# A two-layer diffusion backbone with an RWKV-7 recurrence: small products reordered over the two halves of the array's rows, and key norms broadcast in one pass

## The chip, the cores and the metric

The kernel runs on one core of a Trainium2 chip. The time is device microseconds from the first to the last instruction of one execution; the median of several runs is compared. One execution was profiled, and every row below is from it.

## The reference

Each of two layers takes a stream of 512 tokens (256 of context, 256 latent) by 1024 channels. Three mixers work on one modulated input: multi-head latent attention, a gated short convolution, and a bidirectional RWKV-7 recurrence with 8 heads of 64 channels. They are projected, gated, summed and projected once more; a SwiGLU feed-forward follows. In the recurrence each head and direction keeps a 64 by 64 state:

```
def step(S, inp):
    r_t, w_t, k_t, v_t, kk_t, a_t = inp
    s_kk = jnp.einsum('bhvk,bhk->bhv', S, kk_t)
    S = S * w_t[:, :, None, :] - s_kk[..., None] * (kk_t * a_t)[:, :, None, :] + v_t[..., None] * k_t[:, :, None, :]
    return S, jnp.einsum('bhvk,bhk->bhv', S, r_t)
```

Here `kk` is the key times `k_k`, divided by its norm over the 64 channels of the head. The decay `w` and the rate `a` come from low-rank products (inner width 64), one pair for each direction:

```
w_log = -jax.nn.softplus(-(w0 + jnp.einsum('btzl,zlc->btzc', jnp.tanh(wd), w_up))) - 0.5
a = jax.nn.sigmoid(a0 + jnp.einsum('btzl,zlc->btzc', ad, a_up))
```

## The kernel before

Channels lie on partitions, tokens along the free axis. Large products take weights as an exact sum of two float32r parts (`wload`, L171: ScalarE rounds, VectorE or GpSimd subtracts), so each is three float32r passes (`mm3`, L198 to L201). A float32 product is two passes on TensorE: it shows as two MATMUL records. A scheduler that models the engines sets the order of instructions on each engine when the program is built; each engine then works through its own list in order and waits on semaphores. Tiles of a pool are handed out in the order of the source: a new tile with a tag waits until the last reader of the old one is done.

The recurrence is worked in chunks of 64 tokens. `rwkv_half` (L897) does 256 tokens (a half) in eight units, one for each head pair `hp` and direction `z`. `stage1` (L930) makes a unit's features. For `z == 0` it broadcasts the key norms over the channels of two heads (L934, `sel` times `rnT`) and loads the low-rank weights, which both directions share; then for each `z` it does the low-rank products over 64 of the array's 128 rows: direction 0 has rows 0 to 63, direction 1 rows 64 to 127 (L955 in layer 0 as float32r triples, L957 in layer 1 as float32). They go to bank `c0` or `c1` in layer 0, and to bank `u` for both directions in layer 1. `stage2` (L981) makes the chunk products: for head `e` of the pair (rows 0 to 63, or 64 to 127) four products in a row, one for each chunk `j`, into one of two banks `G` (L1001 to L1006):

```
for e in range(2):
    ps = pr("G", 2)
    for j in range(4):
        pe.matmul(ps[:, j * 128:j * 128 + ncol], FM[r, j], AR[z][r, e, hp, j, 0:ncol], start=True, stop=True)
```

After the eight units comes the inverse of a triangular matrix: a substitution of 62 VectorE operations (L1040 to L1046), then small TensorE products (L1062, L1074), which take their banks from `y` in layer 1. Then comes the scan over four chunks in both directions (L1106 to L1165): for each chunk and direction `Zs` (L1121, copied at L1124), the correction (L1137, negated at L1138 and L1139), the outputs (L1130, L1144) and the new state (L1158, added at L1159, multiplied at L1163 and L1164). The second half's outputs go to DRAM (`yf`, L1167) and come back for the group norm (`Yf`, L1180, transposed at L1186). The products of the input projection, above all those of the gates (L535), stand between all of this on TensorE; I call them gate products. The attention's operands (`dg` at L642, `cqs` at L637) come after the recurrence.

Of the kernel before, what the change touches and what calls it, by code (L numbers as in the profile page):

```python
# [32 lines left out]
# columns of the packed per-channel vectors  # L33
# [10 lines left out]
# order of the 128-column tiles of w_in: name -> index  # L44
M_CQ, M_CKV, M_KR, M_RW, M_CH, M_CB, M_CC, M_GT = 0, 3, 5, 6, 21, 25, 29, 33
# within the recurrence's tiles
R_WD, R_AD, R_K, R_R, R_V, R_GD = 0, 1, 2, 6, 10, 14
NM_IN = 57
# products begun while the first modulated input is made
# [8 lines left out]
# columns of the output that DVE finishes  # L58
# [16 lines left out]
def body(ctx: ExitStack, tc: tile.TileContext, A: dict, out: bass.AP, dbg=None, upto=None):  # L75
# [12 lines left out]
    def pg():  # L88
        """a bank for a product over weights; a phase may lend banks of its own"""
# [25 lines left out]
    # ---------------------------------------------------------------- constants  # L115
# [4 lines left out]
    sel = ct("sel", [128, 128])  # L120
# [34 lines left out]
    # ---------------------------------------------------------------- DRAM scratch  # L155
# [13 lines left out]
    cnt, share = [0], [3]            # every which piece of weights is split by GpSimd  # L169

    def wload(src, shape, pl=None, tag=None, nb=None, to=None):  # L171
        """one piece of weights into SBUF, split exactly into two float32r parts, 512 columns at a time"""
# [30 lines left out]
    def split(src, hi, lo, scale=None):  # L203
        """hi + lo = src * scale"""
# [8 lines left out]
    # ---------------------------------------------------------------- modulation vectors  # L213
    def mod(ps, l, i, kk, j, pl=None):
        """128 columns of vector i of six (shift, scale, gate of either sub-layer) into the rows of slot j"""
# [7 lines left out]
    def mod_out(ps, n):  # L223
        """rows of partial sums of n slots -> columns [128, slot, stream] without their bias"""
# [9 lines left out]
    def mod_rows(l, i, bank=None):  # L234
        """vector i as rows in DRAM, for the token-major gate"""
# [34 lines left out]
    def to_fm(src, tt, h, xf, dst):  # L270
        """half of the columns, token-major -> modulated, transposed, split"""
# [25 lines left out]
    # ---------------------------------------------------------------- layer norm (token-major) of alpha x + g o  # L297
# [5 lines left out]
    def residual(z, acc, gz, xr, stg):  # L303
        """z = alpha x + g o and its mean, variance and inverse deviation per token"""
# [13 lines left out]
    def post(l, sub, accs, stg, dst, res_in, res_out):  # L318
# [1028 lines left out]
```

## Time and profile before

| | us |
|---|---|
| median of 3 runs | 1935.84 |
| the 3 runs | 1932.49, 1935.84, 1936.29 |
| span of the profiled execution | 1933.0 |
| TensorE busy in it | 1843.0 (95%) |
| VectorE busy | 1189.0 (62%) |
| ScalarE busy | 813.9 (42%) |
| GpSimd busy | 518.9 (27%) |
| mean granted TensorE clock | 0.956 of 2.4 GHz |

The profile gives no other time for the profiled execution than its span, which lies 2.8 us below the median of the runs. A busy TensorE is the time in which some matmul was under way, from its start to its modelled end, so that work that overlaps counts once. In the text "layer 0" ends near 1190 us and layer 1 begins there.

### The profile page before, as it was taken

How to read it: one execution, taken by the hardware profiler on the slowest of the kernel's cores; microseconds unless marked ns; L12 is line 12 of the kernel's file. 1: busy time of each engine (PE TensorE's matmuls, PEld its weight loads, DVE VectorE, ACT ScalarE, POOL GpSimd, SP SyncE). 2: the span in 40 equal slices, each digit the busy share in tenths (PEclk: the TensorE clock that was granted, in tenths of full speed). 3: DMA queues.
4: the chain of work that ended last, by engine and by line, in shares of the span. 5: the costliest groups of instructions: out<-in, count | busy, mean ns of one | idle time of the engine just before them, and what ended most of it. 6: DMA issues, size and time to landing. Idle time of an engine off the chain costs nothing. (4 is left out here: it accounts for less than half of the span.)

```text
span 1933.0 us, 35208 instructions
## 1 busy us (share of the span) xinstructions
PE 1843.0 (95%) x13556; PEld 1507.4 (78%) x13556; DVE 1189.0 (62%) x2202; ACT 813.9 (42%) x1736; POOL 518.9 (27%) x614
## 2 busy tenths in 40 slices
PE   7999999999989999999999998999998999979998
PEld 5877777777767767877888887777787896869996
DVE  4578724974457778633333356598978358875665
ACT  2356333534235443333333223465553355535552
POOL 1467113611124223200000016465522133320001
PEclk9998999899989999999999998987899999989999
DMA  8443444244485427433334324453356474566563
GB/s 329 133 142 112 148 130 134 88 137 129 148 284 196 126 62 243 153 131 131 99 98 142 120 87 156 128 145 118 100 180 192 159 257 138 155 232 228 184 231 118
DMA packets 150728, 300.72 MB, mean 156 GB/s; under 512 B 30433, under 2 KB 85793, under 8 KB 150561
## 3 DMA queue, kind: packets, MB, share of 16 engines
q1 hardware_dynamic: 147584, 289.88, 45.9%
q10 hardware_dynamic: 2976, 8.59, 1.3%
q8 instruction: 107, 1.75, 0.4%
q14 instruction: 61, 0.49, 0.1%
HBM read 261.69 MB, written 36.73 MB: 154 GB/s over the span
## 5 line engine op out<-in xcount | busy, mean ns | idle before, releaser
L188 ACT CAST hi<-raw 128x512 fp32r<-128x512 f32 x548 | 331.4, 617 | 553.5 <-PE pg L200 138.7
L189 DVE TENSOR_TENSOR lo<-raw,hi 128x512 fp32r<-128x512 f32 x454 | 331.8, 737 | 371.4 <-ACT hi L188 353.0
L199 PE MATMUL pg<-xh,hi 128*128 128x512 f32 (+1 forms) x912 | 341.3, 376 | 3.5 <-ACT pp L429 2.5
L200 PE MATMUL pg<-xl,hi 128*128 128x512 f32 (+1 forms) x912 | 335.4, 368 | 0.5 <-DVE xl L207 0.5
L201 PE MATMUL pg<-xh,lo 128*128 128x512 f32 (+1 forms) x912 | 334.3, 367 | 0.0
L201 PE MATMUL p_f<-x2h,lo 128*128 128x256 f32 (+1 forms) x688 | 231.9, 337 | 2.2 <-DVE lo L189 2.2
L199 PE MATMUL p_f<-x2h,hi 128*128 128x256 f32 (+1 forms) x688 | 232.7, 338 | 1.0 <-ACT hi L188 1.0
L200 PE MATMUL p_f<-x2l,hi 128*128 128x256 f32 (+1 forms) x688 | 231.6, 337 | 0.6 <-DVE x2l L207 0.6
L189 POOL TENSOR_TENSOR lo<-raw,hi 128x512 fp32r<-128x512 f32 x94 | 126.2, 1343 | 379.5 <-ACT hi L188 345.2
L199 PEld LDWEIGHTS pg<-xh,hi 128*128 128x128 f32 x912 | 183.8, 202 | 35.5 <-issue 6.3
L200 PEld LDWEIGHTS pg<-xl,hi 128*128 128x128 f32 x912 | 184.1, 202 | 26.3 <-issue 3.2
L201 PEld LDWEIGHTS pg<-xh,lo 128*128 128x128 f32 x912 | 183.8, 202 | 23.6 <-issue 1.1
L295 POOL TENSOR_TENSOR rs<-rs,mhalf 128x1 f32<-128x1 f32 x12 | 9.1, 760 | 580.0 <-DVE rs L314 580.0
L199 PEld LDWEIGHTS p_f<-x2h,hi 128*128 128x128 f32 x688 | 131.5, 191 | 16.0 <-ACT hi L188 2.9
L201 PEld LDWEIGHTS p_f<-x2h,lo 128*128 128x128 f32 x688 | 131.4, 191 | 15.8 <-DVE lo L189 2.5
L200 PEld LDWEIGHTS p_f<-x2l,hi 128*128 128x128 f32 x688 | 131.5, 191 | 13.8 <-DVE x2l L207 0.9
L1006 PE MATMUL p_G<-AR,FM 64*128 64x128 f32 x384 | 54.1, 298 | 7.5 <-POOL lo L189 2.4
L613 POOL TENSOR_TENSOR acc<-acc,gts 128x512 f32<-128x512 f32 (+1 forms) x32 | 38.9, 1224 | 82.7 <-DVE gts L611 71.2
L1006 PEld LDWEIGHTS p_G<-AR,FM 64*128 64x128 f32 x384 | 46.8, 200 | 17.9 <-issue 7.6
L990 POOL TENSOR_TENSOR FM<-ta,di 64x256 f32<-64x256 f32 x64 | 53.9, 842 | 23.7 <-PE p_G L1018 15.7
L220 PE MATMUL pg<-raw,cs 128*32 128x128 f32 x1024 | 56.0, 308 | 2.8 <-DMA raw<-in_modw_dram 1.5
L283 ACT ACTIVATE xf<-p_f,modB,modA 128x128 f32<-128x128 f32 x40 | 17.4, 457 | 85.8 <-PE p_f L276 61.2
(391 smaller groups left out, 3678.5 us busy)
## 6 DMA issues: line engine op xcount, KB each, us to landing
raw<-in_win_dram SPq DMA_DIRECT2D x114, 512.0 KB, 4.4
raw<-in_modw_dram SPq DMA_DIRECT2D x96, 512.0 KB, 4.1
raw<-in_w_dram SPq DMA_DIRECT2D x88, 512.0 KB, 3.6
raw<-in_ffn_w_dram SPq DMA_DIRECT2D x44, 512.0 KB, 4.2
raw<-in_wo_dram SPq DMA_DIRECT2D x24, 512.0 KB, 3.5
raw<-in_w_out_dram SPq DMA_DIRECT2D x16, 512.0 KB, 3.6
feat<-nb SPq DMA_DIRECT2D x25, 256.0 KB, 2.6
gate<-gt SPq DMA_DIRECT2D x24, 256.0 KB, 2.8
```

Of the source, the lines that this page charges most:

```text
L188: act.copy(out=hi, in_=r)
L189: e.tensor_tensor(out=lo, in0=r, in1=hi.bitcast(F32), op=ALU.subtract)
L199: pe.matmul(ps, wh, xh, start=first, stop=False, skip_group_check=True)
L200: pe.matmul(ps, wh, xl, start=False, stop=False, skip_group_check=True)
L201: pe.matmul(ps, wl, xh, start=False, stop=last, skip_group_check=True)
L220: pe.matmul(ps[32 * (k % 4):32 * (k % 4) + 32, 0:128], cs[:, o:o + 32], raw[:, k], start=(j == 0 and k < 4), stop=(k >= 4), skip_group_che ...
L283: act.activation(out=xf[:, kk], in_=pt[:, k * 128:(k + 1) * 128], func=ACTF.Identity, scale=modA[:, kk, z:z + 1], bias=modB[:, kk, z:z + 1])
L295: pool.tensor_tensor(out=out_, in0=in_, in1=e, op=ALU.pow)
L613: pool.tensor_tensor(out=a, in0=a, in1=g, op=ALU.add)
L990: pool.tensor_tensor(out=FM[r, :, k0:k0 + 64], in0=rc(ta[r]), in1=rc(Pi[r]), op=ALU.mult)
L1006: pe.matmul(ps[:, j * 128:j * 128 + ncol], FM[r, j], AR[z][r, e, hp, j, 0:ncol], start=True, stop=True)
```

## The change

The chunk products of a unit take both `G` banks at once and alternate between the two heads, that is between the two halves of the array's rows, the upper rows first; `queue_after` adds a dependence without a semaphore, which holds this order in TensorE's list. The low-rank products of both directions are written where `z == 0` is, alternating too, but without such a dependence; they take two banks, `c0` and `c1` in layer 0, and `u` and `y` in layer 1. The key norms are stored as a rounded part and a remainder in four rows, so that one float32r pass over `sel` with four rows adds them. For this `norms` gains a ScalarE copy and two GpSimd operations on 128 x 8 elements for each head pair, and `sel` is loaded through a float32 tile and rounded once.

```
+    def queue_after(later, earlier):
+        tc.add_manual_dep(later.ins, earlier.ins.name,
+                          mybir.DependencyInfo(mybir.DependencyClass.NoSync, mybir.DependencyReason.DATA),
+                          reason="order of issue")
...
-        pow_mhalf(st["rn"][:, :, hp, 0:2], r, 8)
+        pow_mhalf(r, r, 8)
+        h = st["rnh"][:, :, hp]
+        act.copy(out=h, in_=r)
+        pool.tensor_copy(out=st["rn"][:, :, hp, 0:2], in_=h.bitcast(F32))
+        pool.tensor_tensor(out=st["rn"][:, :, hp, 2:4], in0=r, in1=h.bitcast(F32), op=ALU.subtract)
...
-                pe.matmul(pb[:, 0:HT], sel[32 * hp:32 * hp + 2], rnT[32 * hp:32 * hp + 2, h0:h0 + HT], start=True, stop=True)
+                pe.matmul(pb[:, 0:HT], sel[32 * hp:32 * hp + 4], rnT[32 * hp:32 * hp + 4, h0:h0 + HT], start=True, stop=True)
...
+                pus = [pr("u"), pr("y")] if last else [pr("c0"), pr("c1")]
+                zs = (slice(0, 64), slice(64, 128))
+                for i in range(2):
+                    c = slice(i * HT, (i + 1) * HT)
+                    if U3[l]:
+                        for n, (a, b) in enumerate(((0, 0), (0, 1), (1, 0))):
+                            for q, pu in zip(zs, pus):
+                                pe.matmul(pu[:, c], up[q, a, i], wa[q, i, b], start=(n == 0), stop=(n == 2),
+                                          skip_group_check=True)
+                    else:
+                        for q, pu in zip(zs, pus):
+                            pe.matmul(pu[:, c], up[q, i], wa[i][q], start=True, stop=True)
...
-            zz = slice(64 * z, 64 * z + 64)
-            pu = pr("u" if last else f"c{z}")
-            for i in range(2):
-                o = pu[:, i * HT:(i + 1) * HT]
-                if U3[l]:
-                    mm3(o, up[zz, 0, i], up[zz, 1, i], wa[zz, i, 0], wa[zz, i, 1], True, True)
-                else:
-                    pe.matmul(o, up[zz, i], wa[i][zz], start=True, stop=True)
+            pu = pus[z]
...
+            pgs = [pr("G", 2) for e in range(2)]
+            before = None
+            for j in range(4):
+                for e in (1, 0):
+                    r = slice(64 * e, 64 * e + 64)
+                    i = pe.matmul(pgs[e][:, j * 128:j * 128 + ncol], FM[r, j], AR[z][r, e, hp, j, 0:ncol], start=True,
+                                  stop=True)
+                    if before is not None:
+                        queue_after(i, before)
+                    before = i
```

TensorE, layer 0, the chunk products of the third unit of the first half (`p_G`), before:

```order
L201 MATMUL pg_3868<-xh_243,lo_3861 128x512
L199 MATMUL pg_3868<-xh_243,hi_3860 128x512
L1006 MATMUL p_G_1498<-AR0_1287,FM_1487 128x128 x4
L1006 MATMUL p_G_1507<-AR0_1287,FM_1487 128x128 x4
L1018 MATMUL p_y_1516<-ident_69,FM_1487 128x128 x4
L199 MATMUL p_c1_1594<-wa_1278,uhl_1531 128x256
```

The same unit in the changed kernel, with the low-rank products of direction 1 (`p_c1`) ahead of it:

```order
L206 MATMUL pg_3883<-xl_244,hi_3879 128x512
L966 MATMUL p_c1_1550<-wa_1293,uhl_1546 128x256 x5
L1023 MATMUL p_G_1514<-AR0_1302,FM_1502 128x128
L966 MATMUL p_c1_1550<-wa_1293,uhl_1546 128x256
L1042 MATMUL p_y_1610<-ident_69,FM_1581 128x128
L1023 MATMUL p_G_1513<-AR0_1302,FM_1502 128x128
L1023 MATMUL p_G_1514<-AR0_1302,FM_1502 128x128
L1023 MATMUL p_G_1513<-AR0_1302,FM_1502 128x128
L1023 MATMUL p_G_1514<-AR0_1302,FM_1502 128x128
L1023 MATMUL p_G_1513<-AR0_1302,FM_1502 128x128
L1023 MATMUL p_G_1514<-AR0_1302,FM_1502 128x128
L1023 MATMUL p_G_1513<-AR0_1302,FM_1502 128x128
```

The two banks alternate, but the first product stands alone: a product of another tile shape (L1042, 128 rows) comes before the other seven. The low-rank products of direction 1 stand together, five and one. In all, the chunk products were 42 stretches of 8 passes and 11 of 16; now they are 27 of 2, 26 of 14, 5 of 16, one of 8 and one of 6. Stretches of products over 64 rows, low-rank ones included, were 75 and are 85.

TensorE, layer 1, where the low-rank products of direction 1 for the second half's first head pair stand, before (bank `u`, right behind a chunk product of the first half):

```order
L199 MATMUL pg_14114<-xh_10673,hi_14110 128x256
L1006 MATMUL p_G_12030<-AR0a_11627,FM_12021 128x64 x4
L1121 MATMUL p_c1_12392<-SV1_12338,AR1a_11628 64x64
L957 MATMUL p_u_12912<-twd_12870,lw_12888 128x256
L957 MATMUL p_u_12912<-ad_12872,lw_12888 128x256
```

The same products in the changed kernel (bank `y`, L970), among the scan of the first half (L1161, L1182, L1145):

```order
L1161 MATMUL p_c1_12431<-Zs_12429,LBa_11657 64x64 x5
L1182 MATMUL p_c0_12400<-SV0_12361,tml0_12364 64x64 x8
L1161 MATMUL p_c1_12431<-Zs_12429,LBa_11657 64x64 x2
L970 MATMUL p_y_12920<-twd_12898,lw_12916 128x256
L970 MATMUL p_y_12920<-ad_12900,lw_12916 128x256
L206 MATMUL pg_14912<-xl_10689,hi_14908 128x256
```

They moved behind the first half's inverse, which holds bank `y` before them; seven of the second half's eight units follow there, where before all eight stood ahead of that inverse.

TensorE, layer 1, the end of the second half's scan, before (outputs L1144, then gate products from `xh` and `xl`):

```order
L201 MATMUL pg_15530<-xh_10673,lo_15527 128x256
L1144 MATMUL p_y_14030<-LB_12876,SV1_13923 64x64 x7
L199 MATMUL pg_15530<-xh_10673,hi_15526 128x256
L200 MATMUL pg_15530<-xl_10674,hi_15526 128x256
L201 MATMUL pg_15530<-xh_10673,lo_15527 128x256
```

The same place in the changed kernel (outputs L1168, `dg` of the attention L648, keys from `ch`, then the transposes of `Yf` at L1210):

```order
L1154 MATMUL p_y_14058<-AR1_12903,SV1_13951 64x64 x8
L1168 MATMUL p_y_14058<-LB_12904,SV1_13951 64x64 x8
L648 MATMUL p_G_15953<-dg_15969,ones_70 128x128
L205 MATMUL pg_16000<-hi_15992,ch_15972 128x512
L206 MATMUL pg_16000<-lo_15993,ch_15972 128x512
L205 MATMUL pg_16008<-hi_15992,ch_15972 128x512
L206 MATMUL pg_16008<-lo_15993,ch_15972 128x512
L1210 MATMUL p_y_16258<-ident_69,Yf_16256 128x128 x4
```

The gate products are gone from here: before, 153 of them stood between the last output and the transposes of `Yf`, now none does, and none stands in the scan ahead of it either. They moved to earlier places in layer 1, 293 of them in one stretch ahead of the second half's inverse.

## Rows read from the trace of the kernel before

**Rows 1.** The page: busy time of the engines, and TensorE by slices of 48 us.
```profile
PE 1843.0 (95%) x13556; PEld 1507.4 (78%) x13556; DVE 1189.0 (62%) x2202; ACT 813.9 (42%) x1736; POOL 518.9 (27%) x614
...
PE   7999999999989999999999998999998999979998
```

**Rows 2.** Busy time by stretch of layer 1: PE, PEld, DVE, ACT, POOL, granted clock.
```profile
1300.00:1350.00 50.00, 43.75 (x228) 36.28 (x228) 42.25 (x76) 29.67 (x82) 28.57 (x44) 0.77 0.40 124
1350.00:1400.00 50.00, 46.40 (x268) 37.53 (x267) 47.69 (x94) 24.58 (x58) 24.70 (x35) 0.85 0.31 93
1400.00:1450.00 50.00, 48.01 (x682) 43.90 (x682) 37.12 (x76) 25.86 (x51) 13.23 (x17) 0.93 0.57 178
1450.00:1500.00 50.00, 44.49 (x730) 39.77 (x729) 39.35 (x82) 20.75 (x42) 14.12 (x18) 0.97 0.60 188
1500.00:1560.00 60.00, 60.00 (x910) 50.24 (x909) 22.31 (x48) 20.28 (x47) 11.72 (x12) 1.00 0.47 153
```

**Rows 3.** Timeline of TensorE (start, us, form): both heads' chunk products adjacent.
```profile
130.38 1.71 PE L1006 MATMUL p_G<-AR,FM 64*128 64x128 f32 x16
132.01 0.66 PE L1018 MATMUL p_y<-ident,FM 128*128 128x128 f32 x4
```

**Rows 4.** Timeline of TensorE: one head's chunk products alone.
```profile
159.75 1.16 PE L1006 MATMUL p_G<-AR,FM 64*128 64x128 f32 x8
160.84 0.65 PE L1018 MATMUL p_y<-ident,FM 128*128 128x128 f32 x4
```

**Rows 5.** Timeline of TensorE: two passes over 64 rows between others.
```profile
148.05 0.38 PE L199 MATMUL p_c<-wa,uhl 64*128 64x256 f32 x1
148.27 0.28 PE L200 MATMUL p_c<-wa,uhl 64*128 64x256 f32 x1
148.48 0.50 PE L200 MATMUL pg<-xl,hi 128*128 128x512 f32 x1
```

**Rows 6.** Timeline of TensorE: the two passes of a norm broadcast.
```profile
324.04 0.69 PE L934 MATMUL p_c<-rnT,sel 2*128 2x256 f32 x2
324.66 0.50 PE L200 MATMUL pg<-xl,hi 128*128 128x512 f32 x1
```

**Rows 7.** Timeline of TensorE: sixteen-pass groups of the scan, and gate products.
```profile
303.67 0.69 PE L1158 MATMUL p_c<-SV,TM 128*64 128x64 f32 x16
304.29 0.68 PE L1137 MATMUL p_c<-Zs,LB 64*64 64x64 f32 x16
...
1507.43 0.28 PE L199 MATMUL pg<-xh,hi 128*128 128x256 f32 x1
1507.55 0.28 PE L200 MATMUL pg<-xl,hi 128*128 128x256 f32 x1
```

**Rows 8.** Groups by line and shape: VectorE and ScalarE in the scan (busy, mean ns).
```profile
L1124 ACT COPY Zs<-p_c 128x256 f32<-128x256 f32 x32 | 11.9, 372 | 21.6 <-PE p_c L1121 21.3
L1139 DVE TENSOR_SCALAR SV<-p_c 64x256 f32<-64x256 f32 x32 | 13.7, 428 | 27.4 <-ACT SV L1138 26.8
L1159 DVE TENSOR_TENSOR S<-p_c,S 128x256 f32<-128x256 f32 x28 | 11.9, 424 | 29.3 <-PE p_c L1158 28.9 <-PE p_c L1121 0.2
```

**Rows 9.** Timeline of TensorE: last outputs of the scan, and transposes of `Yf`.
```profile
1558.56 0.68 PE L1144 MATMUL p_y<-LB,SV 64*64 64x64 f32 x14
...
1578.47 0.60 PE L642 MATMUL p_G<-dg,ones 128*128 128x128 f32 x4
1578.91 0.38 PE L1186 MATMUL p_y<-ident,Yf 128*128 128x128 f32 x2
```

**Rows 10.** DMA issues: size each, median us from issue to landing.
```profile
yf<-sq SPq DMA_DIRECT2D x3, 512.0 KB, 5.6
Yf<-yf SPq DMA_DIRECT2D x3, 512.0 KB, 7.6
```

**Rows 11.** Busy time in layer 0's second substitution (columns of rows 2).
```profile
399.00:438.80 39.80, 39.05 (x343) 30.28 (x343) 33.68 (x76) 10.12 (x21) 3.91 (x4) 1.00 0.50 159
```

**Rows 12.** Groups by line and shape: a small GpSimd operation.
```profile
L967 POOL COPY fd<-tw 128x4 f32<-128x4 f32 x32 | 11.1, 347 | 5.2 <-ACT tw L966 4.9
```

More of the change, by code (lines that the diff above doesn't have):

```diff
@@ L119, in body @@
     mask = ct("mask", [128, 320])
-    sel = ct("sel", [128, 128])
+    sel = ct("sel", [128, 128], F32R)
     sv = ct("sv", [128, NL, NV])
@@ L879, in norms @@
             st["rn8"] = rt("rn8", [128, 4, 4, 2])
+            st["rnh"] = rt("rnh", [128, 4, 4, 2], F32R)
             pool.memset(st["rn"], 0.0)
@@ L892, in norms_t @@
             pe.transpose(prt[:, t * 128:(t + 1) * 128], rn[:, t].rearrange("p h e -> p (h e)"), ident)
-        rnT = rt("rnT", [128, T])
+        rnT = rt("rnT", [128, T], F32R)
         dve.tensor_copy(out=rnT, in_=prt)
@@ L946, in stage1 @@
                     up = uhl
-                kks[hp] = (kf, kk, fload(R_R + hp, "rr", 2) if read else None, up)
-            kf, kk, rr, up = kks[hp]
-            rv = (lambda a: a) if z == 0 else (lambda a: a[:, ::-1])
-            zz = slice(64 * z, 64 * z + 64)
-            pu = pr("u" if last else f"c{z}")
-            for i in range(2):
-                o = pu[:, i * HT:(i + 1) * HT]
-                if U3[l]:
-                    mm3(o, up[zz, 0, i], up[zz, 1, i], wa[zz, i, 0], wa[zz, i, 1], True, True)
-                else:
-                    pe.matmul(o, up[zz, i], wa[i][zz], start=True, stop=True)
+                pus = [pr("u"), pr("y")] if last else [pr("c0"), pr("c1")]
[10 more added lines that the diff above has]
+                            pe.matmul(pu[:, c], up[q, i], wa[i][q], start=True, stop=True)
+                kks[hp] = (kf, kk, fload(R_R + hp, "rr", 2) if read else None, pus)
+            kf, kk, rr, pus = kks[hp]
+            rv = (lambda a: a) if z == 0 else (lambda a: a[:, ::-1])
+            pu = pus[z]
             tw = rt("tw", [128, HT], bufs=2)
@@ L1003, in stage2 @@
                 o = slice(64 - 64 * e, 128 - 64 * e)
-                ps = pr("G", 2)
-                for j in range(4):
-                    pe.matmul(ps[:, j * 128:j * 128 + ncol], FM[r, j], AR[z][r, e, hp, j, 0:ncol], start=True, stop=True)
-                p4 = ps.rearrange("p (j t) -> p j t", t=128)
+                p4 = pgs[e].rearrange("p (j t) -> p j t", t=128)
                 act.copy(out=LB[64 * e:64 * e + 32, z, hp, :, 0:64], in_=p4[64 * e:64 * e + 32, :, 0:64])
@@ L1262, in start @@
                     sp.dma_start(out=mask, in_=A["mask"])
-                    sp.dma_start(out=sel, in_=A["sel"])
+                    selw = ip.tile([128, 128], F32, tag="selw", name="selw", bufs=1)
+                    sp.dma_start(out=selw, in_=A["sel"])
+                    act.copy(out=sel, in_=selw)
                 for m in range(len(ws)):
@@ L1318, in pack @@
     sel = np.zeros((4, 32, 128), np.float32)
-    sel[:, 0, :64] = 1.0
-    sel[:, 1, 64:] = 1.0
+    sel[:, 0:4:2, :64] = 1.0
+    sel[:, 1:4:2, 64:] = 1.0
     A["sel"] = sel.reshape(128, 128)
```

## The prediction

> **What bounds the kernel now.** I read the page first. TensorE is busy for 1843.0 of 1933.0 us, and the slices show no stretch where it rests for long [rows 1]. So the time is TensorE's own work and 90 us of idling; a saving in TensorE's passes is a saving in time, unless the new order of work opens a wait. Then the timeline of TensorE, for the price of each kind of small product, and last the busy time by stretch of layer 1, because the order changes most there. Between 1300 and 1500 us TensorE idles for 6.25 + 3.60 + 1.99 + 5.51 = 17.35 us, and its granted clock is between 0.77 and 0.97 of full speed; behind it, at 1500 to 1560, it doesn't idle at all and has full clock [rows 2]. The reader is to see there that layer 1 has one stretch with too little TensorE work and one, the scan and the hand-over, that gate products fill. Prices below are from one start to the next, since durations overlap.
>
> **Chunk products.** Sixteen passes, both heads adjacent, took 132.01 - 130.38 = 1.63 us [rows 3], and eight passes of one head 160.84 - 159.75 = 1.09 us [rows 4]. Two passes over 64 rows took 0.43 us [rows 5]. From 2 to 8 passes that is 0.66 us for 6, 0.11 us a pass, with 0.21 us for entering and leaving the 64-row shape. In single file sixteen would be 0.21 + 16 x 0.11 = 1.97 us; they took 0.34 us less, which is three passes of one half beside three of the other where the heads meet. So the halves do run beside each other, and alternation would make this hold for the whole stretch: fourteen passes are seven on each half, 0.21 + 7 x 0.11 = 0.98 us, and sixteen 1.09 us. I take 1.09 us for both, since the half that starts first can't be used up evenly. Before: 42 x 1.09 + 11 x 1.63 = 63.7 us. After, by the counts of the order: 27 x 0.43 + 26 x 1.09 + 5 x 1.09 + 1.09 + 0.87 = 47.4 us (8 passes at their single-file price, 6 likewise). The term is **-16.3 us**. At worst alternation gains no more overlap than the meeting heads have, fourteen passes at 0.21 + 14 x 0.11 - 0.34 = 1.41 us and sixteen at 1.63: 58.4 us and a gain of 5.3. The lone first product of 27 units costs 27 x 0.21 = 5.7 us of the gain; it is in the sum.
>
> Of the Trainium skill, "TensorEngine Tiling (Array Packing)", section "Key Properties", says that different tiles load weights and multiply in parallel, but also that a change of the tiling mode drains TensorE. The trace agrees with the first by the 1.63 us above, and its 0.21 us at the ends of a stretch fits the second. By the drain alone, with the passes in single file, this change would lose: the order has 85 such stretches where there were 75, and the chunk products would take 27 x 0.43 + 26 x 1.75 + 5 x 1.97 + 1.96 = 68.9 us, 5.2 more than now; that is the far end of rival D.
>
> **Norm broadcasts.** Sixteen of them, of two passes each, become one pass. A pair took 324.66 - 324.04 = 0.62 us [rows 6]; half of it is 0.31 us, 16 x 0.31 = **-5.0 us**. If only the pass and none of the entering went, it would be 16 x 0.12 = 1.9, taking 0.12 us as the price of a 256-column pass [rows 7]. The ScalarE copy and two GpSimd operations for each head pair and layer cost TensorE nothing where gate products are at hand: a GpSimd copy of four columns took 0.35 us [rows 12], and the three are a chain of some 1.1 to 1.5 us, once for each layer ahead of `norms_t`. Without cover that would be 3 us in all. The rounding of `sel` is one copy under the first products.
>
> **Low-rank products.** The order realises almost no alternation (six of `c0`, then six of `c1`; in layer 1 a pair of each). I take **-2 us** for fewer broken stretches. The bounds are 0, and full alternation: in layer 0 four head pairs in two halves, six passes of 0.12 us each hidden [rows 7], 8 x 0.72 = 5.8 us; in layer 1 eight times four float32 passes of 256 columns, at twice the 0.11 us of 128 columns [rows 4], 7.0 us; together 12.8. The shown order speaks for the low end.
>
> The three make **-23.3 us**.
>
> **What layer 1 gives back.** There bank `y` is held by the first half's inverse, so seven of the second half's units come behind it, and with them the second scan and the hand-over come later than all gate products.
>
> *The naked scan.* A step's chain is 0.68 + 0.37 + 0.68 + 0.43 + 0.69 + 3 x 0.42 = 4.1 us: two correction products [rows 7], the copy, the negation, the state product, and one addition and two multiplications, all at the addition's price [rows 8]. With hand-overs I estimate 4.4 us. TensorE's work for both directions of a step is ten groups of 0.62 us [rows 7], 6.2 us, so the directions can cover each other, and three inner steps lose little; the first step and the last have no partner. I take **+5 us**, bounds 3 (one chain less what the other direction covers) and 10 (over two chains bare).
>
> *The hand-over.* Before, the last outputs started at 1558.56 us and the transposes of `Yf` at 1578.91 [rows 9], with 153 gate products of 0.12 us, 18.4 us, between. After, the `yf` store (5.6 us) and the `Yf` load (7.6 us) [rows 10] stand bare: 13.2 us, and a little for the copy ahead. TensorE has `dg` and four key products for it, some 2.4 us by pass prices. **+11 us**; 7 if the keys' weights give it more, 13 if these wait too. What is late next is the group norm, and the scores behind it on TensorE.
>
> *The second substitution.* In layer 0 one took 39.8 us with VectorE at 33.68 [rows 11]. In layer 1 after, 293 gate products of 0.12 us, 35.2 us, stand ahead of the inverse, and some products of the late units: **+2 us**, 0 to 6.
>
> *The clock.* At 1300 to 1350 the idling of 6.25 us goes with a granted clock of 0.77, that is with stretches at 1.2 instead of 2.4 GHz [rows 2]. After a bare wait of 11 us small work follows. **+3 us**; none at the least, and 13 if it is as in that window (there 11.5 of 50 us lost).
>
> *The credit.* The gate products that no longer stand in scan and hand-over stand earlier, where TensorE idled for 17.35 us and ran below full clock [rows 2]. Work moved into a wait costs nothing: of these 17.35 us I credit **-13 us**, not all, since VectorE is nearly the limit in a part of it (47.69 of 50 us at 1350). Bounds 0, and 29 with half of the 24 us that the lower clock took there, 50 x (0.23 + 0.15 + 0.07 + 0.03).
>
> Layer 1 thus gives back 5 + 11 + 2 + 3 - 13 = 8 us, and the sum is -15.3 us: 1917.7 us against the profiled 1933.0. That execution lies 2.8 us under the median of the runs, so I forecast 1920.5, **1920 us**.
>
> **The rivals.** A change within 0.2% (3.9 us) is about what a measurement of this kernel can tell from none.
>
> *A, the forecast*, 0.50: alternation as priced, layer 1 gives back 8 us, more or less 11: 1909 to 1931.
>
> *B, nothing is given back*, 0.22. The gate products that move into the idle stretch, and the better clock there, pay for scan and hand-over whole: 1935.8 - 23.3 = 1912. With the credit at 29 it is 8 us less, 1904, and about 1898 with more of the low-rank products alternating. For it speak the 17.35 us of idling and the 24 us of lost clock [rows 2]; against it 13.2 us of transfers that nothing shortens [rows 10]. I put it at 1905.
>
> *C, slower*, 0.14: from the second scan to the transposes of `Yf` the work is one dependent chain, bare and at 1.2 GHz, and what moved ahead of it buys little, because VectorE and not TensorE's list sets the pace at 1300 to 1500. At their bounds the chain's terms are 10 + 13 + 13, with 2 for the substitution 38 us, and the time 1935.8 - 23.3 + 38 = 1950. It decides from where give-back less credit passes 23.3 + 3.9 = 27 us, that is with a credit below 11. VectorE's 47.69 of 50 us at 1350 speaks for it, its 37.12 at 1400 against [rows 2].
>
> *D, it doesn't do what it says*, 0.14: alternating passes overlap no more than adjacent heads did. 5.3 for the chunk products, 5.0 and 2 for the others, 8 given back: 1935.8 - 12.3 + 8 = 1931.5, and 1933.5 without the low-rank part. In single file it would be 1942. Against it stands the overlap where the heads meet [rows 3].
>
> The range of 1900 to 1938 leaves out C and the lower end of B, some 2 in 10. Faster by over 0.2% holds A but for 0.02, B, and half of D: 0.77; within 0.2% 0.10; slower 0.13.
>
> **What the profile after would show.** Stretches of chunk products of 14 passes at about 1.0 to 1.1 us from start to start (D: 1.4), the broadcast line with 16 instead of 32 passes, TensorE's busy time some 20 us lower. In layer 1: fewer idle us and a higher clock where the first half's substitution is, then a second scan without gate products, TensorE idle for some 11 us ahead of the `Yf` transposes, released by the load of `Yf`, and a granted clock below 1 behind it. The forecast fails if a stretch of 14 takes 1.4 us or more, or if the stretch at 1300 to 1500 idles as long as before although it has more gate products.

## The result, and the profile after

The changed kernel took 1955.97 us (median of 4 runs, 1952.28 to 1957.24) beside 1936.07 us for the kernel before (4 runs): a ratio of 1.0096, with a 95% interval of 1.0068 to 1.0124. It is slower, by some 20 us, where 1920 us and a gain were forecast; 1955.97 us lies outside the range too. Of the rivals C, the slower one at 1950 us, came nearest.

The page after: busy time of the engines, and TensorE by slices of 49 us, beside [rows 1].

```profile
PE 1816.6 (93%) x13540; PEld 1483.6 (76%) x13540; DVE 1200.9 (61%) x2202; ACT 812.5 (42%) x1745; POOL 526.3 (27%) x630
...
PE   7998999999979999999999999899898788979998
```

TensorE is busy for 26.4 us less than before, somewhat more than the 23.3 us that the sum took off. But the span is 1954.1 us, so it idles for 137.5 us where it idled for 90.0. The work went, and more waiting came. The timeline of TensorE shows that the prices were right: sixteen passes of chunk products alternating (1.10 us from start to start, 1.63 before), fourteen (1.09 us), and a norm broadcast (0.31 us).

```profile
122.76 0.38 PE L945 MATMUL p_c<-rnT,sel 4*128 4x256 f32 x1
123.07 0.50 PE L205 MATMUL pg<-xh,hi 128*128 128x512 f32 x1
...
129.85 1.16 PE L1023 MATMUL p_G<-AR,FM 64*128 64x128 f32 x16
130.95 0.66 PE L1042 MATMUL p_y<-ident,FM 128*128 128x128 f32 x4
...
156.45 1.16 PE L1023 MATMUL p_G<-AR,FM 64*128 64x128 f32 x14
157.54 0.55 PE L1042 MATMUL p_y<-ident,FM 128*128 128x128 f32 x3
```

So the two halves do run beside each other. Of the Trainium skill, "TensorEngine Tiling (Array Packing)", section "Key Properties", has both the parallel tiles and the drain; the 1.10 us agree with the first, and the second did not take the gain away: a stretch of fourteen is at 1.09 us, not at the 1.75 us of rival D's far end. In all, the 512 passes took 67.5 us before and 49.8 us after, from start to next start and without idle time, so 17.7 us less where 16.3 were forecast.

Busy time by stretch of layer 1 after (columns as in [rows 2]):

```profile
1300.00:1350.00 50.00, 46.51 (x321) 39.51 (x319) 33.69 (x68) 26.16 (x67) 19.06 (x25) 0.91 0.45 148
1350.00:1400.00 50.00, 44.46 (x615) 41.73 (x616) 36.47 (x70) 23.30 (x44) 11.55 (x12) 0.93 0.55 185
1400.00:1450.00 50.00, 43.87 (x447) 36.44 (x448) 45.77 (x76) 24.88 (x65) 29.25 (x46) 0.80 0.42 125
1450.00:1500.00 50.00, 45.24 (x496) 38.09 (x492) 32.01 (x54) 23.80 (x60) 22.99 (x33) 0.97 0.57 179
1500.00:1560.00 60.00, 47.09 (x574) 44.95 (x573) 45.80 (x89) 26.46 (x51) 14.48 (x11) 0.87 0.59 183
```

Between 1300 and 1500 us TensorE idles for 19.92 us (17.35 before), although it has more gate products there (586 passes, before 513), and for 12.91 us in the 60 us behind, where it had not idled. The first of these is one of the two signs by which the prediction itself said that it would fail.

Where the time went is seen by a few starts on TensorE. First the kernel before: the last product of layer 0, the first of layer 1's second inverse, the last gate product; the last outputs of the scan and the transposes of `Yf` are in [rows 9].

```profile
1162.61 0.39 PE L201 MATMUL p_f<-late,hh 128*128 128x512 f32 x1
...
1487.36 0.82 PE L1062 MATMUL p_y<-sq,LB 32*32 32x32 f32 x40
...
1588.71 0.28 PE L201 MATMUL pg<-xh,lo 128*128 128x256 f32 x1
```

The same in the changed kernel, with the last outputs and the transposes:

```profile
1155.44 0.39 PE L207 MATMUL p_f<-late,hh 128*128 128x512 f32 x1
...
1540.71 0.28 PE L207 MATMUL pg<-xh,lo 128*128 128x256 f32 x1
...
1546.68 1.92 PE L1086 MATMUL p_y<-sq,LB 32*32 32x32 f32 x64 [5.70 <-DVE sq L1072]
...
1587.83 1.14 PE L1168 MATMUL p_y<-LB,SV 64*64 64x64 f32 x16 [0.46 <-ACT SV L1162]
...
1599.47 1.05 PE L1210 MATMUL p_y<-ident,Yf 128*128 128x128 f32 x4
```

Layer 0 ends 7.2 us earlier. From there the second inverse begins after 391.2 us, in the kernel before after 324.8: 66.5 us later. From the inverse to the last outputs it takes 41.2 us, before 71.2, because no gate product stands between; from those to the transposes 11.6 us, before 20.4. So the bare scan and the bare hand-over, which I had priced as losses, are 39 us shorter than the covered ones, and the loss was made ahead of them, where I had put a credit. At the transposes layer 1 is 27.7 us behind, and at the end 28.3: 28.3 - 7.2 = 21.1 us of span.

The order on bank `y` shows the place: the last low-rank product of direction 1 for the first half, then the first half's inverse, and behind it the second half's.

```profile
1278.89 0.38 PE L970 MATMUL p_y<-twd,lw 64*128 64x256 f32 x1
1379.03 1.20 PE L1086 MATMUL p_y<-sq,LBa 32*32 32x32 f32 x64 [0.61 <-DVE sq L1072]
...
1395.62 1.20 PE L1098 MATMUL p_y<-LBa,sq 32*32 32x32 f32 x64
1402.32 0.70 PE L970 MATMUL p_y<-twd,lw 64*128 64x256 f32 x2
```

For 123 us no low-rank product of direction 1 is issued. That is what the order showed before; what it costs is read from VectorE. First the kernel before, while the first half's substitution runs; then the changed kernel, the same substitution, and the stretch from the first half's inverse to the second half's substitution (columns as in [rows 2]; VectorE is the third).

```profile
1331.60:1409.30 77.70, 68.58 (x413) 56.07 (x412) 73.51 (x149) 38.82 (x96) 36.80 (x52) 0.87 0.39 118
```

```profile
1332.80:1376.80 44.00, 36.47 (x328) 33.22 (x327) 35.98 (x84) 15.21 (x33) 9.58 (x9) 0.92 0.58 195
1402.30:1502.60 100.30, 89.40 (x924) 75.14 (x921) 79.60 (x131) 50.16 (x128) 52.24 (x78) 0.88 0.50 156
```

Before, the second half's units were made while the substitution ran: beside its own 62 operations, other operations of VectorE, 55.0 us in all, lie in its 77.7 us, and VectorE is nearly full. After, 13.7 us of others lie in its 44.0 us, and the work of seven units follows behind the inverse, in a stretch that is not full (79.60 of 100.30 us). The second substitution starts 347.2 us after layer 0's last product, before 270.8.

### The profile page after: what moved, and what is told of

It is laid out like the page before. It is cut to its first block, busy times and chain, and to the rows that moved or that the text cites. A ratio compares the mean times of both kernels' runs of the same rounds, so it can differ in the third digit from the quotient of the medians.

```text
span 1954.1 us, 35135 instructions
## 1 busy us (share of the span) xinstructions
PE 1816.6 (93%) x13540; PEld 1483.6 (76%) x13540; DVE 1200.9 (61%) x2202; ACT 812.5 (42%) x1745; POOL 526.3 (27%) x630
## 3 DMA queue, kind: packets, MB, share of 16 engines
q8 instruction: 107, 1.75, 0.4%
## 5 line engine op out<-in xcount | busy, mean ns | idle before, releaser
L195 DVE TENSOR_TENSOR lo<-raw,hi 128x512 fp32r<-128x512 f32 x454 | 339.4, 753 | 354.2 <-ACT hi L194 348.6
L205 PE MATMUL pg<-xh,hi 128*128 128x512 f32 (+1 forms) x912 | 335.0, 369 | 14.2 <-DVE modT L258 5.5
L206 PE MATMUL pg<-xl,hi 128*128 128x512 f32 (+1 forms) x912 | 329.9, 362 | 1.2 <-DVE xl L213 1.2
L206 PEld LDWEIGHTS p_f<-x2l,hi 128*128 128x128 f32 x688 | 132.1, 192 | 13.7 <-DVE x2l L213 1.0
L1007 POOL TENSOR_TENSOR FM<-ta,di 64x256 f32<-64x256 f32 x64 | 55.2, 862 | 24.8 <-PE p_G L1042 17.6
L1004 DVE SCALAR_TENSOR_TENSOR FM<-bp,di 64x256 f32<-64x256 f32 x64 | 47.3, 740 | 12.5 <-PE p_G L1042 8.9
L289 ACT ACTIVATE xf<-p_f,modB,modA 128x128 f32<-128x128 f32 x40 | 17.6, 457 | 85.1 <-PE p_f L282 65.8
L1070 DVE TENSOR_TENSOR sq<-sq,iv 128x31 f32<-128x31 f32 (+15 forms) x124 | 50.5, 407 | 3.1
```

What stands on the lines that cost most here:

```text
L195: e.tensor_tensor(out=lo, in0=r, in1=hi.bitcast(F32), op=ALU.subtract)
L205: pe.matmul(ps, wh, xh, start=first, stop=False, skip_group_check=True)
L206: pe.matmul(ps, wh, xl, start=False, stop=False, skip_group_check=True)
L289: act.activation(out=xf[:, kk], in_=pt[:, k * 128:(k + 1) * 128], func=ACTF.Identity, scale=modA[:, kk, z:z + 1], bias=modB[:, kk, z:z + 1])
L1004: dve.scalar_tensor_tensor(out=FM[r, :, b0:b0 + 64], in0=v4(bp[r]), scalar=0.5, in1=v4(Pi[r]), op0=ALU.mult, op1=ALU.mult)
L1007: pool.tensor_tensor(out=FM[r, :, k0:k0 + 64], in0=rc(ta[r]), in1=rc(Pi[r]), op=ALU.mult)
```

## The experiments

Theories, numbered as the expectations use them: (1) bank `y`, taken by direction 1 in layer 1, holds the second half's units back. (2) A unit that claims both `G` banks at once is slower. (3) The norms' longer chain delays the units. (4, 5) VectorE, or the recurrence's chain through it, sets the pace, so passes saved there are worth little. (6) The dependence that pins the alternation makes the first head wait for the second. (7) The wrong head comes first. (8) Layer 1 has a second limit right behind TensorE's work: the recurrence's end and a fixed tail.

Ratios are to the kernel before, run on the same chip in turn. All times in the table but the ratios are of the profiled execution: the start of layer 0's last product, the span from there on ("layer 1"), the starts of layer 1's second inverse (its first TensorE product) and of the last group of scan outputs, and the span from these to the end ("tail").

| kernel | ratio (95%) | span | layer 0 | layer 1 | inverse | outputs | tail |
|---|---|---|---|---|---|---|---|
| before | 1 | 1933.0 | 1162.6 | 770.4 | 1487.4 | 1558.6 | 374.4 |
| changed | 1.0096 (1.0068 to 1.0124) | 1954.1 | 1155.4 | 798.7 | 1546.7 | 1587.8 | 366.3 |
| e1_chunks | 1.0007 (0.9985 to 1.0028) | 1940.7 | 1164.1 | 776.6 | 1500.1 | 1575.0 | 365.7 |
| e2_norms | 0.9980 (0.9958 to 1.0002) | 1937.3 | 1163.4 | 773.9 | 1486.6 | 1561.6 | 375.7 |
| e3_lowrank | 1.0080 (1.0050 to 1.0110) | 1969.3 | 1163.1 | 806.2 | 1526.2 | 1599.5 | 369.8 |
| e4_u_in_layer1 | 0.9994 (0.9972 to 1.0015) | 1936.8 | 1160.7 | 776.1 | 1487.6 | 1562.2 | 374.6 |
| e5_both_banks | 1.0042 (1.0020 to 1.0064) | 1934.8 | 1162.7 | 772.1 | 1481.7 | 1559.1 | 375.7 |
| e6_t_in_u | 1.0089 (1.0054 to 1.0125) | 1949.5 | 1155.7 | 793.8 | 1498.8 | 1575.4 | 374.2 |
| e7_before_t_in_u | 1.0075 (1.0048 to 1.0101) | 1946.6 | 1160.5 | 786.1 | 1494.7 | 1570.0 | 376.6 |
| c1_chunks_norms_u | 1.0101 (1.0070 to 1.0132) | 1956.8 | 1168.4 | 788.4 | 1504.4 | 1581.3 | 375.5 |
| e8_g3_layer0 | 1.0067 (1.0040 to 1.0095) | 1944.5 | 1167.4 | 777.1 | 1501.9 | 1576.7 | 367.8 |
| e12_twice | 1.0306 (1.0269 to 1.0342) | 1996.4 | 1171.4 | 825.0 | 1507.2 | 1579.5 | 416.9 |
| e13_norms_share2 | 0.9958 (0.9936 to 0.9980) | 1928.9 | 1154.5 | 774.4 | 1475.2 | 1552.5 | 376.4 |
| e14_noqueue | 0.9935 (0.9913 to 0.9958) | 1923.5 | 1151.5 | 772.0 | 1475.1 | 1546.3 | 377.2 |
| f1_after_noqueue | 1.0053 (1.0028 to 1.0078) | 1952.1 | 1165.2 | 786.9 | 1532.5 | 1588.0 | 364.1 |
| f2_noqueue_u | 1.0009 (0.9987 to 1.0031) | 1938.0 | 1163.8 | 774.2 | 1482.2 | 1560.1 | 377.9 |
| e10_order01 | 1.0082 (1.0053 to 1.0110) | 1949.8 | 1171.4 | 778.4 | 1507.0 | 1581.5 | 368.2 |
| f3_best | 1.0035 (1.0013 to 1.0058) | 1955.5 | 1170.1 | 785.4 | 1503.4 | 1581.0 | 374.5 |
| e17_gates_two | 1.0001 (0.9981 to 1.0020) | 1932.3 | 1158.3 | 774.0 | 1488.6 | 1564.7 | 367.6 |
| f6_noqueue_share | 0.9997 (0.9980 to 1.0014) | 1936.7 | 1147.7 | 789.0 | 1469.8 | 1550.5 | 386.2 |

A profiled execution can lie 10 to 15 us from its kernel's median (e5_both_banks took 1936.6 us in it, with a median of 1947.1; e3_lowrank 1971.1, with a median of 1956.0), so the ratio gives the verdict and the columns only the place.

### The parts one by one

e1_chunks: the kernel before with the diff's part in `stage2`.

> Only the chunk products alternate; low-rank products and norm broadcasts as before. Theory 1 (the bank y, which low-rank direction 1 takes in layer 1, makes the second half's units wait for the first half's inverse): the saving of 16 us shows nearly whole, 12 to 18 us faster than before, about 1920; the two halves' inverses in layer 1 stay some 70 us apart. Theory 2 (a unit takes both G banks at once, so units follow one another more slowly): 0 to 15 us slower than before, with idle TensorE ahead of chunk products and transposes in layer 1.

e2_norms: the diff's parts in `norms`, `norms_t`, `sel`, and the broadcast of four rows.

> Only the norm broadcast in one pass. Theories 1 and 2 alike: 2 to 5 us faster than before, about 1931 to 1934. Theory 3 (the longer chain of ScalarE and GpSimd ahead of the transposed norms delays all units): 3 to 10 us slower than before.

e3_lowrank: the low-rank products of the diff.

> Only the low-rank products, both directions written together, with bank y for direction 1 in layer 1. Theory 1: all of the loss is here: 30 to 45 us slower than before, 1965 to 1980, with the second scan and the hand-over bare of gate products. Theory 2: within 5 us of before.

e4_u_in_layer1: the whole diff, but

```diff
-                pus = [pr("u"), pr("y")] if last else [pr("c0"), pr("c1")]
+                pus = None
+                if not last:
+                    pus = [pr("u"), pr("y")] if last else [pr("c0"), pr("c1")]
...
-            pu = pus[z]
+            pu = pus[z] if pus else pr("u" if last else f"c{z}")
```

> The whole change, but in layer 1 the low-rank products stand as before (bank u for each direction in its turn). Theory 1: the loss goes and the savings stay: 20 to 28 us faster than before, about 1910 to 1916. Theory 2: about as the changed kernel, 1950 to 1956.

Theory 1 holds for the loss: with the low-rank products alone, `y` among them, the second inverse is at 1526.2 us (e3) and the time 0.80% longer; with everything but `y` the whole 0.96% is gone. The expected 30 us and more of e3 was too much, and the savings of 20 us and more did not show in e4: TensorE is busy for 1817.5 us there, 25.5 less than before, and the time is the same. Theory 3 falls. But neither theory has e1: alternation alone takes 23.1 us off TensorE's busy time (1819.9 us) and gives nothing. Its two inverses in layer 1 stay 71 us apart, as theory 1 has it, but both come 13 us later. One unit of it, in the timeline of TensorE:

```profile
1373.37 0.48 PE L1011 MATMUL p_G<-AR,FM 64*128 64x128 f32 x2
...
1375.17 1.16 PE L1011 MATMUL p_G<-AR,FM 64*128 64x128 f32 x14
...
1382.71 1.09 PE L1030 MATMUL p_G<-ident,FM 128*128 128x128 f32 x4 [3.38 <-DVE AR L1026]
```

The first head's first product stands alone, fourteen passes follow when the other head is ready, and the transposes, which need a `G` bank, wait until VectorE has emptied one: 9.3 us after the unit's first product.

### Why the chunk products give nothing

e5_both_banks keeps the claim and a pinned order, but not the alternation:

```diff
-            for j in range(4):
-                for e in (1, 0):
+            for e in (1, 0):
+                for j in range(4):
```

> Chunk products head after head as before, in eights, but a unit takes both G banks at once and the products over rows 64 to 127 come first, pinned. So TensorE's passes cost what they did before, without the 20 us that alternation took off its busy time. Theory 2 (the claim on both banks lengthens a unit, since a bank is only free after its last evacuation): the units take some 2 us more each as with alternation, and nothing pays for it: 10 to 25 us slower than before. Theory 4 (the saved passes lie where VectorE sets the pace, so they were worth nothing; banks don't matter): within 4 us of before.

e6_t_in_u alternates, and e7_before_t_in_u does not; in both

```diff
-            ps = pr("G", 2) if last else pr("y")
+            ps = pr("u") if last else pr("y")
```

> Chunk products alternate as in the change, and in layer 1 the transposes of FM go to bank u, so that a unit uses G for two tiles and not for three; nothing else. Theory 2: layer 1's units come back to their old pace or better and the saving there shows: 8 to 16 us faster than before, with the first half's inverse in layer 1 at 1400 to 1415 us (1429 with alternation alone). Theory 4: as with alternation alone, within 4 us of before.

> The kernel before with that one move, the transposes of FM in bank u. Control: if G's two banks limited the kernel before as well, 3 to 10 us faster; under theory 2 alone within 4 us, since a head's bank is free again while the other head is worked on.

c1_chunks_norms_u is e6 with the norms of e2.

> Alternating chunk products, the norm broadcast in one pass, the transposes in bank u, and the low-rank products as before. Theory 2: 12 to 20 us faster than before, about 1920. Theory 4: 2 to 6 us faster, the norms alone.

e5 is 0.42% slower, some 8 us, under the 10 that theory 2 expected at least and over the 4 of theory 4; its interval, 4 to 12 us, does not choose. The other three decide nothing on it: the control e7 shows that the move to bank `u` costs 0.75% by itself (`u` also serves the broadcasts and the low-rank products of the next unit, which may be why; no run shows it); that swallowed what e6 was to show, and c1 with it. Beside e7, e6 is no faster.

e8_g3_layer0 gives layer 0 a third `G` bank (it was lent to gate products), here for the chunk products and likewise wherever layer 0 takes a `G` bank:

```diff
-            mix.enter_context(banks(f"psm{l}", 0 if last else 1))
+            mix.enter_context(banks(f"psm{l}", 0))
...
-            pgs = [pr("G", 2) for e in range(2)]
+            pgs = [pr("G", 2 if l == NL - 1 else 3) for e in range(2)]
```

> Chunk products alternate as in the change, layer 1 as with alternation alone; in layer 0 G has three banks in place of two (the third is the one that was lent to the gate products). Theory 2 (banks): layer 0's second inverse comes back towards 439 us, 445 at most (455 with alternation alone), layer 0 ends some us earlier, and the time is 2 to 8 us shorter than with alternation alone. Theory 6 (the two heads' operands are made one after the other, and in alternation the first head waits for the second's, so that both heads' evacuations start late and together): the inverse stays at 450 to 460 and the time within 4 us of alternation alone, or longer for the bank that gate products lose.

e14_noqueue claims both banks and writes the products alternately, without the pin:

```diff
-                    if before is not None:
-                        queue_after(i, before)
```

> The chunk products written alternately and both G banks taken at once, but without the dependence that holds the order: the scheduler then issues one head's four products and the other's four, in eights as before. Theory 2: as slow as the claim on both banks alone, 5 to 12 us slower than before. Theory 6 (pinned alternation makes the first head wait for the second): within 4 us of before, with layer 0's second inverse within 5 us of 439.

e10_order01 keeps the pin and swaps the heads: `for e in (0, 1):`.

> Chunk products alternate, pinned, with rows 0 to 63 first in each pair; nothing else changed. Theory 6: it does not matter which head comes first, since the second product waits for the other head at once: within 4 us of alternation with rows 64 to 127 first. Theory 7 (the rows 64 to 127 come first though their operands are ready last, and that is the loss): 8 to 14 us faster than before.

e14 is the largest gain of the study, 0.65%, and it claims both banks: theory 2 falls as the cause by itself. Where both heads are ready its list alternates, and where not it mostly has four products of one head and then four of the other; stretches of two passes, a product alone, are 5 in its trace and 28 in e1's. A stretch of sixteen, and the three starts of layer 0's end, the last outputs and the last gate product:

```profile
332.21 1.16 PE L1011 MATMUL p_G<-AR,FM 64*128 64x128 f32 x16
333.31 0.66 PE L1028 MATMUL p_y<-ident,FM 128*128 128x128 f32 x4
...
1151.46 0.39 PE L207 MATMUL p_f<-late,hh 128*128 128x512 f32 x1
...
1546.28 0.68 PE L1154 MATMUL p_y<-LB,SV 64*64 64x64 f32 x14
...
1576.56 0.28 PE L207 MATMUL pg<-xh,lo 128*128 128x256 f32 x1
```

So it has the price of 1.10 us without the pin. Beside e1 the last outputs are 28.7 us earlier, 12.6 of them from layer 0. The pin is all that lies between the two kernels, so it is what e1 loses by, 0.72%. Theory 6 has the place right: the first products of layer 0's second inverse end at 438.0 us in e14, 439.2 before and 455.5 in e1. It has not the size: it expected a time within 4 us of before, and e14 is 8 to 17 us faster. That the pin costs by the first head's wait is read from the unit above and not tested apart. A third bank (e8) made the time longer, but there the same products end at 446.7 us, between what the two theories expected, so the banks may have a part in the pin's cost. Theory 7 falls with e10, which is slower than e1 by 0.75% where theory 6 expected no difference: to swap the heads moves the time as much as to drop the pin.

### The pin inside the whole change

f1_after_noqueue and f2_noqueue_u are the changed kernel and e4 without the two lines above.

> The whole change without the dependence that pins the alternation (both banks still taken at once, low-rank products and norms as in the change). Theory 6 (the pin holds the first head back until the second is ready): 8 to 16 us faster than the changed kernel, that is within 0.5% of before on the slow side; the loss that is left is bank y's in layer 1. If the pin costs only together with the single saving it brings (theory 2, banks): within 4 us of the changed kernel.

> As the run before, and in layer 1 the low-rank products as before, in bank u. Theories 1 and 6 together: both losses are gone, 12 to 20 us faster than before. Theory 1 alone: as with the pin, within 4 us of before.

Without the pin the changed kernel comes from 1.0096 to 1.0053, some 8 us, the least that was expected, and taking `y` away as well gives 1.0009. But f2 is no faster than e4, its like with the pin: the gain of e14 did not come back beside the norms and layer 0's low-rank products. In f1 and f2 the first products of layer 0's second inverse end at 457.4 and 456.7 us, as late without the pin as e1's with it. So to drop the pin is not enough there.

### What bounds the kernel

e12_twice issues each chunk product twice:

```diff
-                    pe.matmul(ps[:, j * 128:j * 128 + ncol], FM[r, j], AR[z][r, e, hp, j, 0:ncol], start=True, stop=True)
+                    for again in range(2):
+                        pe.matmul(ps[:, j * 128:j * 128 + ncol], FM[r, j], AR[z][r, e, hp, j, 0:ncol], start=True, stop=True)
```

> The kernel before, with every chunk product issued twice (the second writes the same values again): some 512 passes more, by 0.11 us 56 us of TensorE work in the stretches where the units' features are made. If TensorE's own work bounds the kernel there, as the prediction had it: 45 to 60 us slower. Theory 5 (the recurrence's chain through VectorE and ScalarE sets the time in layer 1, and TensorE has slack and lower clock in those stretches): 10 to 30 us slower.

e17_gates_two leaves out one of three passes of layer 1's gate products, those with the input's remainder, so its gates are less exact:

```diff
-            mm3(ps[:, c0:c1], wh(k), wl(k), xh[:, k, c0:c1], xl[:, k, c0:c1], k == 0, k == 7)
+            if l == NL - 1 and M_GT <= m < M_GT + 24:
+                pe.matmul(ps[:, c0:c1], wh(k), xh[:, k, c0:c1], start=(k == 0), stop=False, skip_group_check=True)
+                pe.matmul(ps[:, c0:c1], wl(k), xh[:, k, c0:c1], start=False, stop=(k == 7), skip_group_check=True)
+            else:
+                mm3(ps[:, c0:c1], wh(k), wl(k), xh[:, k, c0:c1], xl[:, k, c0:c1], k == 0, k == 7)
```

> The kernel before, with one of the three passes of layer 1's gate products left out (the weights' rounded part times the input's remainder): 192 passes of 0.12 us, 23 us less TensorE work in layer 1, and nothing else removed. If TensorE's own work is the limit, as the prediction had it: 18 to 25 us faster. Theory 8 (two limits in layer 1: TensorE's gate products and, some 9 us behind them, the end of the recurrence with a fixed tail of 365 to 368 us): at most 5 to 11 us faster, the last gate product ends some 20 us earlier, the last scan output no earlier than 393 us after layer 0's end, and the tail from there falls from 373.8 to 365 to 370 us.

The two together are the answer. 512 passes more cost 59 us; 192 passes less, 23 us of work, gave 0.0%. TensorE's work is a limit from one side alone. (Of e12's loss most is in layer 1: gate products came to stand behind the scan, the last at 1658.4 us, and the tail is 416.9 us. That is no slack as theory 5 had it.) In e17 the last gate product starts 17.6 us earlier than before and the tail shrinks to 367.6 us, as theory 8 has it; and the last outputs come 6.2 us later, which it left open. Its last outputs and last gate product:

```profile
1564.73 0.68 PE L1148 MATMUL p_y<-LB,SV 64*64 64x64 f32 x16
...
1571.08 0.28 PE L393 MATMUL pg<-xh,lo 128*128 128x256 f32 x1
```

The stretch of layer 1's units, in the kernel before, in e17_gates_two and in e12_twice, one fence each (columns as in [rows 2]):

```profile
1250.00:1430.00 180.00, 167.81 (x1172) 141.16 (x1171) 157.21 (x278) 104.64 (x258) 91.83 (x140) 0.82 0.44 131
```

```profile
1250.00:1430.00 180.00, 167.56 (x1066) 138.82 (x1065) 153.26 (x272) 100.12 (x248) 89.45 (x133) 0.77 0.41 129
```

```profile
1250.00:1430.00 180.00, 162.25 (x882) 139.73 (x880) 130.77 (x236) 82.95 (x210) 77.22 (x123) 0.67 0.28 84
```

VectorE is busy for 157 of 180 us there before. In e17 the same busy time of TensorE holds 106 fewer passes, at a lower clock. So a lower clock is a rival account of why e17 gained nothing, and it holds beyond this stretch: the mean granted clock of e17's 12 runs is between 0.947 and 0.953, that of the kernel before, on the same chip, between 0.954 and 0.964. The page of e17 sets the two beside each other: of the 23 us taken out, TensorE's busy time fell by 17.4 (to 1825.6), and its idle time rose by 16.7 (to 106.7). So most of the saving became waiting, and the smaller part, some 6 us, went to the clock or to overlap.

e13_norms_share2, f3_best and f6_noqueue_share move splits of weights off VectorE in layer 1's recurrence, on e2, on e14 with e2's norms, and on e14:

```diff
-SHARE = ((3, 3, 0), (3, 5, 0))
+SHARE = ((3, 3, 0), (2, 5, 0))
```

> The norm broadcast in one pass alone, and in layer 1's recurrence every second piece of weights is split by GpSimd, not every third: some 24 us of work leave VectorE. Theory 5: VectorE paces the units there, so the last scan output of layer 1 comes 5 to 12 us earlier after layer 0's end, and the time is 4 to 10 us shorter than with the norms alone. If VectorE's load does not matter: within 4 us of the norms alone.

> Chunk products as written in the change without the pin, the norm broadcast in one pass, the low-rank products as before, and in layer 1's recurrence every second piece of weights split by GpSimd. If the gains of the parts add: 16 to 24 us faster than before. If they fill the same gap: 8 to 14 us faster.

> Both G banks at once and the chunk products alternating as written, without the pin, and in layer 1 every second piece of weights split by GpSimd; norms and low-rank products as before. If the two gains add: 14 to 20 us faster than before. If their sum depends on where the scheduler puts the recurrence, as in f3: anywhere within 10 us of before, and the time follows the last scan output of either layer.

e13 is 0.42% faster, 0.2% more than the norms alone, in the overlap of both intervals; the profile has the gain over e2 in layer 0, where the two are written alike (1154.5 and 1163.4 us), and not in layer 1. So the expectation of theory 5 is not met. f3 and f6 show that gains don't add: f3 joins three edits that gained or were neutral and is 0.35% slower than before, f6 joins two and is where before was.

## Why the prediction was wrong

**The step that failed first** is in the first paragraph: "a saving in TensorE's passes is a saving in time". I had taken TensorE's 95% for the bound, and counted 23.3 us for the passes. With all of these savings and without `y` (e4) TensorE is busy for 25.5 us less, idles for 119.3 us where it idled for 90.0, and the time is the same (0.9994, 0.9972 to 1.0015). e17 took 23 us of other passes away and gave nothing. Over all 20 traces, layer 1 is never shorter than the 770.4 us of the kernel before. The rows suggest why: the shortest tails, from the last outputs of the scan to the end, are 364 to 368 us, and before it was 374.4 us. So I take the end of the recurrence for a second limit, 6 to 10 us behind TensorE's work, that did not come earlier with fewer passes (1562.2 us in e4, 1564.7 in e17, before 1558.6). This is read across single executions; no run moves that end alone. I read the idle time between 1300 and 1500 us, and VectorE's 47.69 of 50 us beside it [rows 2], and trimmed the credit for it, but still priced the passes as if nothing else were near the limit.

**The credit of -13 us** had the wrong sign, and with it the 8 us that layer 1 was to give back: `y` costs 1.0% with the pin (changed kernel against e4), 0.44% without (f1 against f2). What moved ahead of the second inverse did not fill waits: that inverse came 66.5 us later, since VectorE's work for seven units, which had run beside the first half's substitution, lay behind the first half's inverse. The front part had shown this move; I priced the place it left (scan, hand-over) and not the place it went to. e4 and f2 without `y` have the inverse at 1487.6 and 1482.2 us, where it was.

**The naked scan (+5) and the hand-over (+11)** were no losses to the chain that ends last: from inverse to transposes it became 38.8 us shorter. TensorE does idle there, for 6.8 and 5.8 us, but its gate products had only stood in the way.

**The chunk products** were sized right as TensorE's work (49.8 us after where the sum has 47.4, 67.5 before where it has 63.7; the busy time fell by 26.4 in all). The 0.43 us for two passes was read from passes of 256 columns, where the lone first products have 128; these took 0.41 us in the median. But the pin was taken for free. I counted the lone first product as 0.21 us of entering; it also holds a bank, and the first head's evacuation waits for the second head. In e1, with the pin, both inverses of layer 1 are 13 us later; in e14, without it, they are 16 and 12 us earlier than before, 11 of them from layer 0. The Trainium skill, "TensorEngine Tiling (Array Packing)", section "Restrictions and Gotchas", says that different row tiles write to different PSUM banks, so alternation asks for two at a time. By e14 the claim alone was no loss; both heads in one bank were not tried.

**Right** were the norm broadcast (0.31 us a pass, and a ratio of 0.998, near the -5 us, within an interval that reaches 1.0002), the low-rank products' missing alternation, and rival C's place in time. Of C's mechanism one half was right, that what moves ahead of the scan buys little because VectorE sets the pace there; the other was not, since scan and hand-over were bare, but shorter. So C's 1950 us is in part luck.

**Open.** Why e14's gain is lost beside other edits (f2, f3, f6) isn't settled, nor how much of the pin's cost in e1 is the first head's wait. e7 changes one bank of four transposes and costs 0.75%, and e10 swaps two heads and costs as much. Each edit gives another list on every engine, and the last outputs lie between 1546 and 1600 us; that these lists, not the edits' own work, make the differences of some tenths of a per cent is argued from this and not shown by a run.

## What to carry to other kernels

A busy share of 95% does not say that less work means less time: ask what ends next, here, by my reading, the chain of the recurrence plus its tail, and take the gap to it (an estimate of 6 to 10 us) as the most that a saving on the first limit alone can bring. When a change moves work past a bank's holder, follow the engine that feeds the moved work (VectorE, for seven units), and price the place it goes to. Write an order, but doubt a pin if its members aren't ready together: the same sixteen-pass stretch of 1.10 us came without the pin, and that version, e14_noqueue, is the fastest here (0.9935, 0.9913 to 0.9958). To drop the pin was worth 0.72% alone and 0.43% in the whole change, but nothing in e4.

## What I had not expected of the hardware

In the stretch of the units TensorE's busy time hardly shows the granted clock: 0.82 before, 0.77 with fewer gate passes (e17), 0.67 with chunk products issued twice (e12), at busy times of 167.8, 167.6 and 162.3 of 180 us. As the clock has the two levels of 1.2 and 2.4 GHz here, these means are some 36, 46 and 66% of the time at the lower one. In both experiments the stretch holds fewer passes than before (1172, then 1066 and 882): e17 has fewer gate passes, and e12 has 160 chunk passes more, but half of the gate products have left it. Which of the two the clock follows can't be read from these rows. The windows are the same 180 us of each execution, while layer 0's end lies at 1162.6, 1158.3 and 1171.4 us.
